# The low parts of a decoder trunk's attention weights subtracted on VectorE instead of GpSimd

## The chip, the cores and the metric

The kernel runs on one core of one Trainium2 chip. The metric is device microseconds of one execution; three executions of the kernel before took 1800.78 us in the median (1799.58 to 1805.04). The profiled execution is a run of its own. Engine names are those of the profile: PE is the matrix engine, PEld its weight loads, DVE is VectorE, ACT is ScalarE, POOL is GpSimd, SP is the queue that issues most DMAs.

## The reference, cut to what matters

Two layers over 1024 tokens of width 1024, all float32: an RWKV-7 layer and a differential-attention layer, each followed by a gated per-layer embedding, and a last RMSNorm. The change touches the attention layer:

```python
def diff_attn_mixer(h, w_in, lq1, lk1, lq2, lk2, subln, w_out, lambda_init):
    proj = h @ w_in                                   # q, k, v and gate of 8 heads
    q, k, v, gate = jnp.split(proj, [...], axis=-1)
    q, k = rope(q, cos, sin), rope(k, cos, sin)
    def block(args):                                  # 128 queries
        s = jnp.einsum('bhcqd,bhckd->bhcqk', qi, kt) * scale
        pr = jax.nn.softmax(causal(s), axis=-1)       # two maps per head
        att = pr[:, :, 0] - lam * pr[:, :, 1]
        return jnp.einsum('bhqk,bhkd->bhqd', att, vt)
    o = rms_norm(o, subln, DA_SUBLN_EPS) * (1.0 - lambda_init)
    return (o.reshape(B, S, DA_WIDTH) * jax.nn.silu(gate)) @ w_out
```

## The kernel before, in words

Every large product is computed in three matmuls of a rounded format (`mm3`): each operand x is split into a high part h, which ACT rounds by a copy, and a remainder x - h, which a second engine subtracts; then h·h, h·l and l·h are added in PSUM. The function `split(hi, lo, src, lo_eng)` does it: one ACT copy, and one subtraction on `lo_eng` (POOL where none is named). The subtraction reads two tensors of SBUF, the source and the high part.

The attention part works in nine passes of eight steps (`step(ph, ah, i)`). Pass `ph` projects head `ph`, 128 tokens a step (`pmm`: 24 matmuls of 512 columns into a tile called `qkv`, in two halves), while the head before, `ah = ph - 1`, goes through scores (`sc`), exponentials (`e`), the two maps' combination (`combine`, again `e`), transposition (`at`, evicted to SBUF by DVE as `aT`), the product with the values (`av`), and norms (`finish`, small rows on a 128x2 tile `ost`). Each step also rotates q and k (`rp`, `rq`: two rows on DVE, the rest on POOL), scales the gate (`sg`) and transposes q and k (`qkt`). The last pass, 8, has no projection; it loads the output projection's rows (`dwo`) and multiplies with them (`do`).

The weights of a head are four rows of 128x1024 (`dw` followed by head and row: dw43r is the raw row 3 of head 4, without the r the split one), the output projection has eight (`dwo0r` to `dwo7r`). Raw rows have two buffers (`RAW`), so the DMA of a row starts when the subtraction of the row two before it has ended. Head 0's rows are split in the last step of the stage before (the list `dw0`); the rows 0, 1 and 2 of head `ph + 1` are loaded in steps 2 to 4 of pass `ph` and row 3 in its last step (`wload2`); the rows of the output projection are loaded at the same places of the last two passes (`wo_row`). In the order that results, the four splits of a head run together at the end of one pass and the beginning of the next: row 3 of one head, then rows 0, 1 and 2 of the head after it.

The stage before the attention ends with `post2` of the last token tile: rows called `ple07th`, `h1b`, `da6`, `da7` and `n2r`, and the transposed and split activations `hT`. At the attention's start five small loads are issued on SP behind the write of `h1b`, among them `lamt`, from which a scalar `nlam` is computed on DVE.

The order of the instructions on each engine in this part is not the order of the code: a list scheduler inside the tile framework sets it, from its own model of durations and from priorities by program order, so a change of an engine moves other rows as well. Each engine then runs its own list in order.

Of the kernel before, what the change touches and what calls it, by code (L numbers as in the profile page):

```python
# [37 lines left out]
def trunk(ctx: ExitStack, tc: tile.TileContext, A, out):  # L38
# [17 lines left out]
    V, S, G, T = engines = [Engine(e) for e in (nc.vector, nc.scalar, nc.gpsimd, nc.tensor)]  # L56
# [29 lines left out]
    def split(hi, lo, src, lo_eng=None):  # L86
        S.activation(hi, src, AF.Copy)
        (lo_eng or G).tensor_tensor(out=lo, in0=src, in1=hi.bitcast(F32), op=ALU.subtract)
# [644 lines left out]
    def slot(nm):  # L733

        q = nslot[0] % RB
        nslot[0] += 1
        if q < 4:
            t = tip.tile([P, 2, D], F32R, tag=f"ti{q}", name=nm)
        else:
            t = de.tile([P, 2, D], F32R, tag="r", name=nm, bufs=RB - 4)  # L740
        return t[:, 0], t[:, 1]

    def wrow(nm, src, own=None, scale=None, lo_eng=None, raw=None, load=True):
        r = de.tile([P, D], F32, tag="raw", name=nm + "r", bufs=RAW) if raw is None else raw
        if load:
            nc.sync.dma_start(out=r, in_=src)
        if own is None:
            h, lo = slot(nm)
        else:
            h, lo = own  # L750
        if scale is None:
            split(h, lo, r, lo_eng)
        elif lo_eng is not None:
            S.activation(r, r, AF.Copy, scale=scale)
            split(h, lo, r, lo_eng)
        else:
            S.activation(h, r, AF.Copy, scale=scale)
            V.scalar_tensor_tensor(out=lo, in0=r, scalar=scale, in1=h.bitcast(F32), op0=ALU.mult, op1=ALU.subtract)
        return h, lo
# [86 lines left out]
    RB, RAW = 7, 2  # L846
# [6 lines left out]
    def big(kt, x, nm, dt=F32R):  # L853
        return dw.tile([P, D], dt, tag=f"b{kt}{x}", name=nm, bufs=1)

    with NB("d") as d, NP("psco") as pp:
# [108 lines left out]
        def wo_row(kt):  # L965
            r = wo_raw.pop(kt)
            h, lo = big(kt, 0, f"rwo{kt}h"), big(kt, 1, f"rwo{kt}l")
            split(h, lo, r, V)
            wo[kt] = (h, lo)
# [123 lines left out]
        for c in range(NCH):  # L1093
            i, odd = (c - 2) // 2, c % 2
# [39 lines left out]
            if c == 1:  # L1134
                wo_row(0)
            if c == 2:
                wo_row(5)
# [87 lines left out]
        def pre2(i):  # L1225
            h1 = d2.tile([P, D], F32, tag="h", name=f"h1b{i}", bufs=3)
            nc.sync.dma_start(out=h1, in_=h1_d[i * P:(i + 1) * P, :])
            for cs in GS:
                if i == cs.start:
                    RS[0] = group_rs(rn.rearrange("p c h j -> p c (h j)"), ss1, cs)  # L1230
            rs = RS[0][:, i:i + 1]
            n = dt_("y", f"n{i}", 3) if i < 2 else dt_("sg" if i % 2 else "xr", f"n{i}")
            V.tensor_scalar(out=n, in0=h1, scalar1=rs, scalar2=None, op0=ALU.mult)
            gh = kview(dt_("gh", f"ph{i}", 2, F32R))
            gl = kview(dt_("gl", f"pl{i}", 2, F32R))
            transpose_split(pp, f"ptr{i}", n, lambda hf: gh[:, hf * 4:hf * 4 + 4], lambda hf: gl[:, hf * 4:hf * 4 + 4],
                            tag="t")
            D2[i] = (h1, gh, gl)

        def mms2(i):  # L1240
            h1, gh, gl = D2[i]
            def tick(n, j=i - 2):
                if j > 0 and j % 2 and n in TT and n2p[j]:
                    kp = n2p[j].pop(0)
                    turn2(j, pp, "us", (D2[j - 1], D2[j]), [kp])
            D2[i] = (h1, proj_N(pp, f"pg{i}", gh, gl, wg, ("xy", "mm")[i % 2], 2, i == NT - 1, tick=tick))

        def post2(i):
            h1, pss = D2[i]
            rows = slice(i * P, (i + 1) * P)  # L1250
            ss = ple_tail(lambda tag, nm: dt_(tag, nm), d, f"ple0{i}", pss, h1, pp_d[0][rows, :])
            nc.sync.dma_start(out=h2_d[rows, :], in_=h1)
            rs = rms_rs(d, f"da{i}", ss, D, 1e-6)
            if i == NT - 2:
                nring.extend(t.bitcast(F32) for t in slot("n2r"))
            n2 = dt_("y", f"n2{i}", 3) if i < NT - 2 else nring[i - NT + 2]
            V.tensor_scalar(out=n2, in0=h1, scalar1=rs, scalar2=None, op0=ALU.mult)
            D2[i] = n2
# [39 lines left out]
        dw0 = []  # L1298
        TT = (2, 4, 6, 8)
        n2p = {j: list(range(KT // 2)) for j in (1, 3, 5)}  # L1300
        for i in range(1, NT):
            mms2(i)
            if i == NT - 1:
                for k4 in range(4):
                    hh, ll = slot(f"dw0{k4}")
                    split(hh, ll, dw0[k4], (G, G, V, G)[k4])
                    dw0[k4] = (hh, ll)
            if i + 2 < NT:
                pre2(i + 2)
            post2(i)  # L1310
            if i == NT - 3:
                dw0 = [de.tile([P, D], F32, tag="raw", name=f"dw0{k4}r", bufs=RAW) for k4 in range(2)]
                dw0 += [dt_("lnw", "dw02r"), dt_("y", "dw03r", 3)]
                for k4 in range(4):
                    nc.sync.dma_start(out=dw0[k4], in_=A["dqkvg"][0, k4])
# [5 lines left out]
    with tc.tile_pool(name="at", bufs=1, reuse_waits="tile") as at, tc.tile_pool(name="psat", bufs=1, space=PSUM, reuse_waits="tile") as pp:  # L1321
# [26 lines left out]
        def wload2(h, k4, lo_eng):  # L1348
            r = de.tile([P, D], F32, tag="raw", name=f"dw{h}{k4}r", bufs=RAW)
            nc.sync.dma_start(out=r, in_=A["dqkvg"][h, k4])  # L1350
            hh, ll = slot(f"dw{h}{k4}")
            split(hh, ll, r, lo_eng)
            H[h]["w"].append((hh, ll))
# [146 lines left out]

        def wo_row(kt):
            wo.append(wrow(f"dwo{kt}", A["dwo"][:, kt],
                           None if kt < RB else (big(0, 0, "dwo7h"), big(0, 1, "dwo7l")), lo_eng=V if kt in (4, 6) else G))

        def eturn(i):
            og = big(1, i % 2, f"og{i}", F32)
# [14 lines left out]
        def emm(i, hf):  # L1521
            gh, gl = EE[i]
            cs = slice(hf * 512, hf * 512 + 512)
            ps = pp.tile([P, 512], F32, tag="mm", name=f"do{i}{hf}", bufs=2)
            for kt in range(7):
                mm3(ps, gh[:, kt], gl[:, kt], wo[kt][0][:, cs], wo[kt][1][:, cs], kt == 0, kt == 6)
            V.tensor_tensor(out=h3[i][:, cs], in0=ps, in1=h3[i][:, cs], op=ALU.add)
# [38 lines left out]
        def step(ph, ah, i):  # L1566

            last = ph == DH
            if ah >= 0:
                scores(ah, i)  # L1570
            if i == 0 and ph > 1 and not last:
                pend.pop(1)()
            if not last:
                pmm(ph, i, 0)
                if i == NT - 1 and ph + 1 < DH:
                    wload2(ph + 1, 3, V)
            else:
                for kt in ((3, 4, 5, 6), (7,))[i] if i < 2 else ():
                    wo_row(kt)
                if i:  # L1580
                    emm(i - 1, 0)
            late = pend[1:] + pend[:1] if last and i == 0 else pend[:]
            del pend[:]
            for f in late:
                f()
            if ah >= 0:
                combine(ah, i)
            if not last:
                pmm(ph, i, 1)
                if ph == 0 and i == 2:  # L1590
                    turn2(NT - 1, pp, "tr", n7)
                if i and i % 2 == 0:
                    qkt(ph, i - 2)
                if i == NT - 1:
                    pend.append(lambda: qkt(ph, i - 1))
                if 2 <= i < 5:
                    if ph + 1 < DH:
                        if i == 2:
                            head(ph + 1)
                        wload2(ph + 1, i - 2, G)  # L1600
                    else:
                        wo_row(i - 2)
            else:
                e7 = range(3 * i - 18, 3 * i - 15) if i >= 6 else ()
                for x in e7:
                    turn7(x)
                if i == 0:
                    eturn(0)
                else:
                    emm(i - 1, 1)  # L1610
                if i in (3, 5, 7):
                    gate_pair(len(wg1), {3: "k1", 5: "kv", 7: "k1"}[i])
                if i == 7:
                    gate_pair(3, "q1")
                for x in e7:
                    emm7(x)
                if i + 1 < NT:
                    eturn(i + 1)
            if ah >= 0:
                pend.append(lambda: values(ah, i))  # L1620
                if i % 2:
                    pend.append(lambda: finish(ah, i - 1, 2))
# [127 lines left out]
```

## Time and profile before

| | |
|---|---|
| three timed executions, median | 1800.78 us (1799.58 to 1805.04) |
| profiled execution | 1792.27 us |
| its span, first to last instruction | 1790.4 us |
| PE busy | 1676.9 us, 94% |
| DVE busy | 1272.1 us, 71% |
| ACT busy | 798.9 us, 45% |
| POOL busy | 609.0 us, 34% |
| chain that ended last | PE 63%, DVE 25%, issue 4%, ACT 4%, POOL 3%, DMA 1% |

Busy times are sums over an engine's instructions, so overlapping ones count once. "Idle before" in a row is the time in which the engine did nothing before that row, and behind the arrow stands what ended it. In the profile nearly all rows carry the line of one helper (L50), so they are told apart by the tiles that they write and read: `dw<-dw43r,dw` is the subtraction for row 3 of head 4, and the copy before it is `dw<-dw43r`. Buffer numbers are left out there. A matmul or transposition of plain float32 operands shows as two records. Matmul ends are modelled.

### The profile page before, as it was taken

The page shows a single profiled execution, that of the slowest core. Times are in us where ns is not written, and L with a number is a line of the kernel's source. Part 1 is how long each engine was busy: PE and PEld are TensorE (multiplying, and loading weights), DVE is VectorE, ACT ScalarE, POOL GpSimd, SP SyncE. Part 2 cuts the span into 40 slices and gives each one's busy share as a digit, 9 for nine tenths or more (in the row PEclk, how much of TensorE's full clock was granted, in tenths as well). Part 3 has the DMA queues.
Part 4 walks back from the last instruction along what each step waited for, and adds up shares of the span by engine and source line. Part 5 has one row for each costly group of instructions (what it writes and reads, how often), then busy time and mean ns, then how long its engine had stood idle before and what let it go on. Part 6 is the DMA issues. An engine that isn't in the chain of part 4 may idle for free.

```text
span 1790.4 us, 31127 instructions
## 1 busy us (share of the span) xinstructions
PE 1676.9 (94%) x11768; PEld 1391.3 (78%) x11768; DVE 1272.1 (71%) x2910; ACT 798.9 (45%) x1690; POOL 609.0 (34%) x647
## 2 busy tenths in 40 slices
PE   6899999898998989999899899899999999999998
PEld 5677778887677878887678778788888888777786
DVE  7865845698994476666756657887787887856665
ACT  6567743346344443334434344444444444444332
POOL 4433634224323455656300342332423323311200
PEclk9999999998898999999899999999999999999999
DMA  7115444434216553453523210110111101521122
GB/s 261 53 54 165 140 121 104 131 99 117 82 62 192 168 172 119 131 167 113 212 101 135 93 60 7 53 49 17 54 33 30 56 9 55 188 70 34 59 95 71
DMA packets 164404, 176.03 MB, mean 98 GB/s; under 512 B 74845, under 2 KB 127837, under 8 KB 164254
## 3 DMA queue, kind: packets, MB, share of 16 engines
q1 hardware_dynamic: 161950, 169.84, 30.6%
q10 hardware_dynamic: 2304, 4.20, 0.6%
q8 instruction: 93, 1.52, 0.4%
q14 instruction: 57, 0.47, 0.1%
HBM read 124.19 MB, written 49.81 MB: 97 GB/s over the span
## 4 chain that ended last, share of the span: by engine, by line
PE 63%; DVE 25%; issue 4%; ACT 4%; POOL 3%; DMA 1%; SPq 0%; ACTq 0%; DVEq 0%; POOLq 0%
PE qkv L50 18%; PE d L50 7%; PE fg L50 5%; PE pg L50 5%; PE do L50 4%; PE sc L50 3%; DVE xmt L50 3%; PE xy L50 3%; PE av L50 3%; DVE tm L50 3%; PE op L50 3%; DVE tb L50 3%; DVE nb L50 2%; DVE ost L50 2%; PE pm L50 1%
## 5 line engine op out<-in xcount | busy, mean ns | idle before, releaser
L50 ACT ACTIVATE e<-sc,mx 128x256 f32<-128x256 f32 (+7 forms) x128 | 94.1, 739 | 110.7 <-DVE mx L50 59.7
L50 POOL TENSOR_TENSOR rp<-rp,rq 128x128 f32<-128x128 f32 x128 | 61.7, 503 | 227.8 <-DVE rq L50 173.8
L50 PE MATMUL sc<-k,q 128*128 128x512 f32 (+2 forms) x384 | 88.7, 363 | 3.8 <-ACT e L50 2.2
L50 PE MATMUL av<-vh,aT 128*128 128x128 f32 x576 | 81.2, 281 | 6.3 <-DVE aT L50 6.3
L50 PEld LDWEIGHTS av<-vh,aT 128*128 128x128 f32 x576 | 75.6, 195 | 12.8 <-DVE aT L50 8.9
L50 POOL TENSOR_TENSOR m<-m,mmask 128x512 f32<-128x512 f32 x32 | 47.9, 1496 | 81.7 <-ACT m L50 81.7
L50 DVE TENSOR_REDUCE mxs<-sc 128x1 f32<-128x128 f32 (+6 forms) x112 | 73.9, 680 | 0.5
L50 PEld LDWEIGHTS sc<-k,q 128*128 128x128 f32 x384 | 63.2, 190 | 12.9 <-ACT e L50 3.0
L50 PE MATMUL pg<-pwg,ph 128*128 128x512 f32 x224 | 73.2, 405 | 0.0
L50 PE MATMUL do<-dwo,oh 128*128 128x512 f32 x224 | 71.7, 401 | 0.8 <-DVE h L50 0.6
L50 DVE SCALAR_TENSOR_TENSOR xmt<-hT,cB,xmt 128x512 f32<-128x512 f32 x64 | 63.6, 1011 | 6.2 <-ACT xmt L50 5.8
L50 ACT ACTIVATE o<-av,r 128x128 f32<-128x128 f32 x64 | 23.5, 368 | 90.1 <-PE av L50 89.9
L50 DVE TENSOR_TENSOR tm<-tb,nb 128x31 f32<-128x31 f32 (+15 forms) x124 | 57.1, 461 | 3.6
L50 DVE SCALAR_TENSOR_TENSOR e<-e,r,e 128x128 f32<-128x128 f32 (+3 forms) x64 | 56.7, 887 | 1.2
L50 POOL CAST q<-q 64x128 fp32r<-64x128 f32 x128 | 38.8, 304 | 52.2 <-PE sc L50 48.0
L50 POOL CAST k<-k 64x256 fp32r<-64x256 f32 x64 | 25.7, 401 | 84.6 <-ACT k L50 83.5
L50 DVE TENSOR_TENSOR tb<-tb,tm 128x31 f32<-128x31 f32 (+15 forms) x124 | 51.8, 417 | 3.6
L50 DVE TENSOR_TENSOR rp<-qkv,rc 128x256 f32<-128x256 f32 x64 | 27.0, 421 | 36.7 <-PE qkv L50 34.0
L50 DVE COPY aT<-at 128x512 f32<-128x512 f32 (+2 forms) x96 | 51.8, 549 | 1.1 <-PE at L50 0.4
L50 PE MATMUL at<-ident,e 128*128 128x128 f32 x288 | 47.4, 277 | 3.1 <-DVE e L50 2.6
L50 DVE SCALAR_TENSOR_TENSOR ost<-ost 128x2 f32<-128x2 f32 x192 | 47.4, 247 | 3.8
L50 DVE TENSOR_TENSOR m<-pm,mmask 128x512 f32<-128x512 f32 x32 | 22.1, 691 | 38.2 <-PE pm L50 38.1
(1136 smaller groups left out, 5602.7 us busy)
## 6 DMA issues: line engine op xcount, KB each, us to landing
pp_d<-ppo SPq DMA_DIRECT2D x32, 256.0 KB, 2.5
kb_d<-kb SPq DMA_DIRECT2D x16, 512.0 KB, 3.3
kkr<-kkr_d SPq DMA_DIRECT2D x32, 256.0 KB, 3.8
kb<-kb_d SPq DMA_DIRECT2D x32, 256.0 KB, 3.5
x<-in_x SPq DMA_DIRECT2D x8, 512.0 KB, 5.8
kkr_d<-ep SPq DMA_DIRECT2D x16, 256.0 KB, 2.6
kkr_d<-rt SPq DMA_DIRECT2D x16, 256.0 KB, 2.6
bb<-kb_d SPq DMA_DIRECT2D x32, 128.0 KB, 2.9
```

What stands on the lines that cost most here:

```text
L50: r = f(*a, **k)
```

## The change

Of the 40 split weight rows of the attention (32 of the projections, 8 of the output projection) DVE subtracted 10 and POOL 30: three of head 0, three of each of seven other heads, six of the output projection. Now DVE subtracts all 40. Copies, loads, tiles and buffers are the same.

```diff
@@ last step of the stage before the attention
                 for k4 in range(4):
                     hh, ll = slot(f"dw0{k4}")
-                    split(hh, ll, dw0[k4], (G, G, V, G)[k4])
+                    split(hh, ll, dw0[k4], V)
                     dw0[k4] = (hh, ll)
@@ def wo_row(kt), rows of the output projection
             wo.append(wrow(f"dwo{kt}", A["dwo"][:, kt],
-                           None if kt < RB else (big(0, 0, "dwo7h"), big(0, 1, "dwo7l")), lo_eng=V if kt in (4, 6) else G))
+                           None if kt < RB else (big(0, 0, "dwo7h"), big(0, 1, "dwo7l")), lo_eng=V))
@@ def step(ph, ah, i)
                         if i == 2:
                             head(ph + 1)
-                        wload2(ph + 1, i - 2, G)
+                        wload2(ph + 1, i - 2, V)
                     else:
                         wo_row(i - 2)
```

The scheduler places the new rows among DVE's others and moves rows on PE, DVE, ACT and SP from the stage's last step on. First place: DVE where pass 3 ends and pass 4 begins, before the change. The tile `aT_12828` is the one for which PE's `av` waits there, `aT_12890` is the next transposition.

```order
L50 TENSOR_TENSOR dw_12814<-dw43r,dw_12814 128x1024
L50 SCALAR_TENSOR_TENSOR ost_10784<-ost_10784 128x2
L50 TENSOR_TENSOR ost_10784<-ost_10784 128x2
L50 SCALAR_TENSOR_TENSOR ost_10784<-ost_10784 128x2 x2
L50 COPY aT_12828<-at_12824 128x384
L50 TENSOR_TENSOR ost_10784<-ost_10784 128x2
L50 RECIPROCAL r_12957<-l_12868 128x2
L50 SCALAR_TENSOR_TENSOR ost_10784<-ost_10784 128x2
L50 SCALAR_TENSOR_TENSOR r_12957<-r_12957,l_12868,nlam 128x1
L50 SCALAR_TENSOR_TENSOR ost_10784<-ost_10784 128x2
L50 SCALAR_TENSOR_TENSOR e_12876<-e_12883,r_12957,e_12876 128x128
L50 TENSOR_SCALAR ost_10784<-ost_10784 128x2
```

Behind these come `rp`, two rows `o`, `rq` and then `aT_12890`. The same place on DVE with the change, from the same row on.

```order
L50 TENSOR_TENSOR dw_12814<-dw43r,dw_12814 128x1024
L50 SCALAR_TENSOR_TENSOR ost_10784<-ost_10784 128x2
L50 TENSOR_TENSOR dw_13163<-dw50r,dw_13163 128x1024
L50 SCALAR_TENSOR_TENSOR ost_10784<-ost_10784 128x2
L50 COPY aT_12828<-at_12824 128x384
L50 RECIPROCAL r_12957<-l_12868 128x2
L50 TENSOR_TENSOR ost_10784<-ost_10784 128x2
L50 TENSOR_TENSOR rp_12858<-qkv_12799,rc 128x256
L50 TENSOR_TENSOR rq_12859<-qkv_12799,rsn 128x256
L50 SCALAR_TENSOR_TENSOR r_12957<-r_12957,l_12868,nlam 128x1
L50 SCALAR_TENSOR_TENSOR ost_10784<-ost_10784 128x2
L50 COPY aT_12890<-at_12885 128x512
```

The subtraction of dw50r now stands ahead of `aT_12828`, the rows `rp` and `rq` stand ahead of `aT_12890`, and the two rows `o` have gone behind it; the subtractions of dw51r and dw52r come 9 and 15 rows after the last of these, behind the `sg` row that frees the `qkv` tile. Second place: PE at the same boundary with the change, where the second pair of `qkt` transpositions stood behind the matmuls of `hT4` before and now stands behind the first pair.

```order
L50 MATMUL av_12830<-vh_10783,aT_12828 128x128 x3
L50 MATMUL at_12892<-ident,e_12786 128x128 x4
L50 MATMUL qkt_12925<-ident,rp_12749 128x128 x2
L50 MATMUL qkt_12925<-ident,rp_12858 128x128 x2
L50 MATMUL av_12899<-vh_10783,aT_12890 128x128 x4
L50 MATMUL qkv_12912<-dw_12371,hT0h 128x512 x2
```

PE so needs the rotated tile `rp_12858`, which POOL finishes, before it begins the first projection of the pass. Third place: DVE at the end of the stage before the attention, before the change; the tiles `da6` are a row's norm, and `n2r` is scaled with it.

```order
L50 TENSOR_SCALAR da6r<-da6r 128x1
L50 SCALAR_TENSOR_TENSOR hT2l<-htr_10009,vecs,hT2h 128x256
L50 SCALAR_TENSOR_TENSOR da6t<-da6r,da6m 128x1
L50 SCALAR_TENSOR_TENSOR hT1l<-htr_9994,vecs,hT1h 128x256
L50 SCALAR_TENSOR_TENSOR da6r<-da6t,da6r 128x1
L50 SCALAR_TENSOR_TENSOR da6t<-da6r,da6m 128x1
L50 SCALAR_TENSOR_TENSOR da6r<-da6t,da6r 128x1
L50 SCALAR_TENSOR_TENSOR hT3l<-htr_10009,vecs,hT3h 128x256
L50 SCALAR_TENSOR_TENSOR da6t<-da6r,da6m 128x1
L50 SCALAR_TENSOR_TENSOR da6r<-da6t,da6r 128x1
L50 TENSOR_SCALAR n2r<-h1b_9704,da6r 128x1024
L50 TENSOR_TENSOR dw_10078<-dw02r,dw_10078 128x1024
```

Behind these stand the `ple07th`, `hT` and `h1b` rows of the last tile. The same place with the change, behind the subtraction of dw00r and its `hT` rows:

```order
L50 TENSOR_SCALAR da6r<-da6r 128x1
L50 TENSOR_TENSOR dw_10075<-dw01r,dw_10075 128x1024
L50 SCALAR_TENSOR_TENSOR da6t<-da6r,da6m 128x1
L50 TENSOR_TENSOR dw_10078<-dw02r,dw_10078 128x1024
L50 SCALAR_TENSOR_TENSOR hT3l<-htr_10009,vecs,hT3h 128x256
L50 SCALAR_TENSOR_TENSOR da6r<-da6t,da6r 128x1
L50 TENSOR_TENSOR dw_10081<-dw03r,dw_10081 128x1024
L50 SCALAR_TENSOR_TENSOR da6t<-da6r,da6m 128x1
L50 TENSOR_TENSOR dw_10311<-dw10r,dw_10311 128x1024
L50 SCALAR_TENSOR_TENSOR da6r<-da6t,da6r 128x1
L50 TENSOR_TENSOR dw_10351<-dw11r,dw_10351 128x1024
L50 SCALAR_TENSOR_TENSOR ple07th<-ple07th,ple07pp 128x512
```

Six subtractions now stand ahead of the last tile's `ple07th` and `h1b` rows, where one did, and `n2r` has gone behind these.

## Rows read from the trace of the kernel before

**Rows 1.** Stretches of the span; columns as in the first line.
```profile
core 0: us, PE busy (x) PEld busy (x) DVE busy (x) ACT busy (x) POOL busy (x), PEclk, DMA share, GB/s
990.00:1019.00 29.00, 24.37 (x105) 19.20 (x104) 23.55 (x47) 13.13 (x27) 13.34 (x10) 0.94 0.42 143
1019.00:1041.00 22.00, 20.19 (x96) 16.21 (x96) 8.20 (x22) 7.09 (x21) 7.12 (x14) 1.00 0.07 25
1118.00:1133.00 15.00, 9.76 (x53) 8.60 (x52) 14.68 (x35) 7.02 (x18) 9.30 (x9) 0.78 0.36 113
1266.20:1274.20 8.00, 6.15 (x46) 5.38 (x45) 7.86 (x25) 3.51 (x9) 5.19 (x6) 1.00 0.44 147
1274.20:1335.80 61.60, 61.60 (x320) 51.71 (x319) 48.74 (x161) 27.24 (x84) 17.82 (x39) 1.00 0.08 24
1543.00:1569.00 26.00, 21.69 (x123) 16.99 (x122) 23.29 (x74) 14.50 (x37) 9.32 (x13) 1.00 0.86 318
```

**Rows 2.** PE's largest wait from 985 to 1570 us: total, times, longest.
```profile
PE qkt L50 <- DVE aT L50: 8.1, 6, 1.4
```

**Rows 3.** Timeline of DVE where pass 3 ends: start, duration, instruction.
```profile
1265.32 0.16 DVE L50 SCALAR_TENSOR_TENSOR ost<-ost 128x2 f32<-128x2 f32 x1
1265.40 1.22 DVE L50 TENSOR_TENSOR dw<-dw43r,dw 128x1024 fp32r<-128x1024 f32 x1
1266.54 2.33 DVE L50 SCALAR_TENSOR_TENSOR ost<-ost 128x2 f32<-128x2 f32 x1
...
1269.49 0.56 DVE L50 COPY aT<-at 128x384 f32<-128x384 f32 x1
...
1270.22 0.22 DVE L50 SCALAR_TENSOR_TENSOR r<-r,l,nlam 128x1 f32<-128x1 f32 x1
...
1272.01 0.68 DVE L50 COPY aT<-at 128x512 f32<-128x512 f32 x1
...
1275.49 2.32 DVE L50 SCALAR_TENSOR_TENSOR r<-r,l,nlam 128x1 f32<-128x1 f32 x1
```

**Rows 4.** POOL's subtractions there: duration in ns, start in us.
```profile
L50 POOL TENSOR_TENSOR dw<-dw50r,dw x1: 2718/2718/2718, 1266.1 to 1266.1; 128x1024 fp32r<-128x1024 f32 x1
L50 POOL TENSOR_TENSOR dw<-dw52r,dw x1: 2386/2386/2386, 1275.4 to 1275.4; 128x1024 fp32r<-128x1024 f32 x1
```

**Rows 5.** Timeline of PE in the same stretch.
```profile
1272.83 0.41 PE L50 MATMUL qkt<-ident,rp 128*128 128x128 f32 x2 [1.36 <-DVE aT L50]
```

**Rows 6.** Timeline of DVE as the attention begins.
```profile
999.89 2.33 DVE L50 SCALAR_TENSOR_TENSOR da6r<-da6t,da6r 128x1 f32<-128x1 f32 x1
1002.26 2.81 DVE L50 TENSOR_SCALAR n2r<-h1b,da6r 128x1024 f32<-128x1024 f32 x1
...
1009.11 0.67 DVE L50 SCALAR_TENSOR_TENSOR h1b<-ple07th,h1b 128x512 f32<-128x512 f32 x1
```

**Rows 7.** PE and SP there.
```profile
1006.26 0.50 PE L50 MATMUL qkv<-dw,hT4h 128*128 128x512 f32 x1 [2.92 <-DVE dw L50]
...
1012.78 0.33 SPq L1333 DMA_DIRECT2D lamt<-in_lam  x1
...
1018.25 0.73 PE L50 MATMUL qkv<-dw,hT0h 128*128 128x512 f32 x2 [1.70 <-DVE sg L50]
```

**Rows 8.** DVE, ACT, POOL and PE where pass 1 ends.
```profile
1120.00 2.32 DVE L50 SCALAR_TENSOR_TENSOR ost<-ost 128x2 f32<-128x2 f32 x1
...
1123.99 1.06 ACT L50 ACTIVATE dw<-dw31r 128x1024 fp32r<-128x1024 f32 x1
...
1125.28 3.37 DVE L50 SCALAR_TENSOR_TENSOR e<-e,r,e 128x1024 f32<-128x1024 f32 x1
...
1127.51 1.28 POOL L50 CAST q<-q 64x128 fp32r<-64x128 f32 x1
...
1128.70 1.97 PE L50 MATMUL at<-ident,e 128*128 128x128 f32 x8 [2.62 <-DVE e L50]
```

**Rows 9.** ACT's wait for a landing where pass 2 ends.
```profile
1198.92 1.06 ACT L50 ACTIVATE dw<-dw41r 128x1024 fp32r<-128x1024 f32 x1 [2.51 <-DMA dw41r<-in_dqkvg]
```

## The prediction

> **What bounds the kernel now.** I read the table of stretches first, cut at the places where the profile's list of waits names PE. Between two pass ends PE has no idle time at all: 61.60 us busy of 61.60, while DVE is busy for 48.7 [rows 1]. A faster DVE or POOL is worth nothing there. PE waits only in short stretches: 1.85 us (8.00 less 6.15) where pass 3 ends [rows 1], the same within 0.01 at the ends of passes 2, 4, 5 and 6 (five in all); 5.2 us where pass 1 ends, 4.6 as the attention begins, 1.8 shortly after, 4.3 in the last pass [rows 1]. Together that is 25.2 us, the most that this change can win apart from the clock. In these stretches DVE is full: 7.86 of 8.00, 14.68 of 15.00.
>
> The list of waits says what PE waits for: the eviction `aT` on DVE, 8.1 us in six waits for the `qkt` that takes the freed bank [rows 2], 1.36 us of the 1.85 at one pass end [rows 5].
>
> Then the timeline of DVE, for why `aT` is late. At 1266.54 a row `ost` on 128x2 elements takes 2.33 us, where the same row took 0.16 just before; at 1275.49 a row `r` on 128x1 takes 2.32, where one took 0.22 [rows 3]. Both lie inside a subtraction of POOL: dw50r runs from 1266.1 for 2.72 us, dw52r from 1275.4 for 2.39, and each stretched row ends as POOL's does [rows 4]. The pair stands at all five pass ends of this kind, and the first row of it lies ahead of `aT`. So a subtraction that is no concern of PE holds DVE up for 2.2 us at the moment when PE needs DVE. The same lies over `n2r`, 2.81 us, and `da6r`, 2.33 [rows 6], and over `ost` and `e` where pass 1 ends [rows 8].
>
> **The change part by part.** Removed: 30 subtractions of 2.35 to 2.7 us on POOL [rows 4], and with them the stretches. Added: 30 on DVE at 1.22 us each, of which the next row sees 1.14 (1265.40 to 1266.54) [rows 3]. DVE so gets 34.2 us of work. A pass end has three of them, 3.4 us, and loses 2.17 + 2.10 = 4.3 of stretch; with 9.3 as the attention begins, 6.4 where pass 1 ends and 3.4 in the last pass the 20 stretched rows make 40 us. What counts is what stands ahead of each eviction.
>
> *Ends of passes 3 to 6, four times.* The order shows `ost`, the subtraction of dw50r, `ost`, then `aT`. From 1266.54: 0.20 + 1.14 + 0.20 puts the first `aT` at 1268.1 instead of 1269.49 [rows 3], and PE's wait for it (the other 0.49 of the 1.85) is gone. For the second `aT`, `rp` and `rq` now stand ahead, the two `o` rows no longer do: 1268.1 + 0.48 + some 1.4 for seven rows gives 1270.0 instead of 1272.01, with up to half a microsecond more if POOL's rotation holds the small rows up. PE reaches that `qkt` at about 1271.0 (1272.83 less 1.36 less 0.49 [rows 5]), so the 1.36 goes too, but for 0.2. The other two subtractions stand behind `sg`, which frees the next projection's bank: PE has 24 matmuls ahead of it by then. The early second `qkt` needs POOL's rotation, which ends at about 1270.6; it costs 0 to 0.3. I take 1.65 a pass end, 6.6 us.
>
> *End of pass 2.* The same, but dw41r stands ahead of `sg` there, and it comes only after its copy, which waited for a landing until 1198.92 [rows 9]. The projection then starts about 0.9 us late. I take 0.8 of 1.85.
>
> *End of pass 1.* `ost` loses 2.2, dw30r adds 1.14; `e`, 3.37 us long, loses a stretch of the same kind, some 2.1, and nothing stands in its place [rows 8]. So `e` ends at about 1125.4 instead of 1128.65. PE waited 2.62 us for it at 1128.70 [rows 8]; what is late next is the copy of dw31r at 1123.99, which waits for a landing and holds the exponential behind it. I take 3.0 of the 5.2.
>
> *As the attention begins.* Six subtractions instead of one now stand ahead of `h1b`: 5 x 1.14 = 5.7 us more. Five stretched rows go, together 9.3 us, with `n2r` and `da6r` [rows 6] the largest, and `n2r` moves behind. `h1b` at 1009.11 ends about 4 us earlier, and so do the loads on SP behind it, `lamt` at 1012.78 among them, on which PE's third projection at 1018.25 hangs through `sg`. PE's stall at 1006.26 (2.92) goes, but a wait for `lamt` of about 2.3 us stays [rows 7]. I take 3.7, from 0 (the copy of dw11r may land late, and its subtraction stands ahead of `h1b`) to 4.6.
>
> *Shortly after* (1019 to 1041): `qkt` moves ahead of a projection and the scores find their operands ready; 1.0 of the idle 1.8 [rows 1].
>
> *End of pass 0:* PE does not wait there, and DVE's spare time hides the four subtractions; they cost 0, or 1.1 if one comes late and stands before the rows that free a bank.
>
> *Last pass:* three subtractions add 3.4 us to a stretch in which DVE is busy for 23.3 of 26.0 [rows 1]; two of them stand ahead of score and `do` operands for which PE waits, and would cost 2.3. At most the idle 4.3 can be won. I take 0, between the two.
>
> Sum: 6.6 + 0.8 + 3.0 + 3.7 + 1.0 = 15.1 us. The profiled execution took 1792.27 us, 1.9 more than its span; it becomes 1777.2. The timed median, 1800.78, lies 8.5 above that execution, and I carry the difference over: 1786.
>
> *The clock.* Where PE had waited, the granted clock was below full in the next microseconds: 0.78 over the 15 us where pass 1 ends, 0.94 as the attention begins, 1.00 at the other pass ends of the rows [rows 1]. That is up to 3.3 and 1.7 us of PE time. If the waits go, some of it may come back; none is in the sum.
>
> *A rule weighed.* POOL's rows are held up as well: a `q` cast took 1.28 us beside the end of the stretched `e` [rows 8]. The new subtractions can do that to POOL's casts and rotations, and can be held up by them. The Trainium skill (SBUF — State Buffer, Who interferes with whom) says that the port pair is an exclusive lock between a DVE instruction with two SBUF inputs and a GpSimd one that reads SBUF, taken by whichever issues first. The stretched rows here agree, two-input ones all but `n2r`. By that rule each new row may wait behind a small POOL row, an estimate of at most 0.9 us (a rotation's two rows), and delay one by up to 1.1. I count neither: POOL's rows have microseconds of slack except the one `qkt` above.
>
> **The rivals.**
>
> *No change (within 5 us).* DVE only swaps 40 us of stretches for 34 of subtractions, and what PE waits for next is just behind: the landing of the middle rows. ACT's copy of dw41r waited 2.51 us for it [rows 9], and copies stand on ACT ahead of `o`, the casts and the exponentials. For it: DVE's busy time hardly falls. Against it: the stretch sits ahead of `aT` and the middle subtractions behind it. It would leave the pass ends at 1.85 and win only at the beginning: 0 to 5 us, 1796 to 1801. The Trainium skill (Perfetto Trace Analysis, Optimizing Scalar/DVE Operations) says the same in general: offloading between GpSimd and DVE might not help, since they share a port. By that rule this rival holds; the rows so far speak for the other, because POOL's subtraction takes 2.4 us and DVE's 1.2.
>
> *Slower.* DVE is the engine that ends PE's waits, and subtractions now stand ahead of `aT`, `sg` and `h1b`. If the small rows' 2.3 us were not POOL's doing, they stay, and each subtraction in front of an eviction adds 1.14 to a wait that is already there: one or two at seven pass ends (8 to 16 us) and five ahead of `h1b` (up to 5.7): 13 to 22 us, 1814 to 1823. It decides as soon as more than two subtractions precede the second `aT`, or a stretched row stays without a POOL row beside it. Against it: each stretched row ends with POOL's.
>
> *Much faster.* All idle time goes and the clock stays full: 25 + 5, 1771.
>
> **How the numbers follow.** The forecast 0.74 (its own range 1778 to 1794), no change 0.15, slower 0.06, much faster 0.05. A difference under 0.3%, 5.4 us, could not be told from none. Faster than 1795.4: the forecast but for a small tail, and the last case, 0.78. Slower than 1806.2: 0.07. Between: 0.15. The range leaves out the slower case, the upper end of no change, and the extreme win: 1775 to 1799.
>
> **What would show it.** Right: `ost` and `r` at the pass ends back at 0.16 and 0.22; DVE's busy time down by about 6 us, POOL's by 73; PE's idle time at the ends of passes 3 to 6 below 0.4 us; PE's waits for `aT` (8.1 us for `qkt`) under 2; `lamt` issued about 4 us earlier. Wrong step by step: `aT` at a pass end not earlier (the order would have eaten the gain), a long wait of PE on `sg` or `qkt` at every pass end (the middle subtractions or POOL's rotation late), or the last pass longer by over 2.4. Wrong altogether: rows of 2.3 us on DVE without a POOL subtraction beside them.

## The result, and the profile after

The changed kernel took 1775.8 us in the median (1772.86 to 1780.80; one disturbed run of 4070.86 us is left out), the kernel before 1800.18 us in the same series: 24.4 us between the medians where 15.1 were forecast. The ratio is 0.9884, 95% interval 0.986 to 0.9907, that is, 16.7 to 25.2 us; the forecast lies just below that. The profiled spans are 1770.7 and 1790.4 us, 19.7 apart. A second series of the same two kernels gave 0.987 (0.9847 to 0.9893).

These are the stretches of the changed kernel that answer to [rows 1]. It reaches the attention 2.8 us later and the end of the last pass 16.9 earlier, so the windows are shifted to the same work:

```profile
core 0: us, PE busy (x) PEld busy (x) DVE busy (x) ACT busy (x) POOL busy (x), PEclk, DMA share, GB/s
993.00:1022.00 29.00, 27.71 (x129) 22.30 (x128) 20.72 (x56) 14.20 (x30) 2.36 (x6) 1.00 0.44 143
1022.00:1044.00 22.00, 22.00 (x106) 18.03 (x105) 11.10 (x27) 7.48 (x23) 7.16 (x16) 1.00 0.08 25
1113.30:1128.30 15.00, 11.98 (x73) 10.09 (x72) 13.57 (x44) 8.27 (x22) 2.64 (x7) 1.00 0.44 149
1254.50:1262.50 8.00, 7.54 (x54) 6.77 (x53) 7.97 (x26) 4.00 (x12) 1.52 (x5) 1.00 0.44 138
1262.50:1324.10 61.60, 61.60 (x322) 51.85 (x321) 50.25 (x166) 26.95 (x84) 14.22 (x36) 1.00 0.08 26
1526.00:1552.00 26.00, 22.40 (x123) 17.95 (x122) 23.17 (x73) 16.06 (x38) 5.52 (x11) 0.93 0.91 334
```

PE's idle time at the end of pass 3 is 0.46 us (8.00 less 7.54) instead of 1.85, as the attention begins 1.29 instead of 4.6, where pass 1 ends 3.0 instead of 5.2. The granted clock is 1.00 in the two windows that had 0.94 and 0.78; the last pass, 1.00 before, now has 0.93.

DVE at the end of pass 3, beside [rows 3] (start, duration, instruction):

```profile
1255.13 1.22 DVE L50 TENSOR_TENSOR dw<-dw50r,dw 128x1024 fp32r<-128x1024 f32 x1
1256.26 0.15 DVE L50 SCALAR_TENSOR_TENSOR ost<-ost 128x2 f32<-128x2 f32 x1
1256.45 0.56 DVE L50 COPY aT<-at 128x384 f32<-128x384 f32 x1
...
1257.72 0.21 DVE L50 SCALAR_TENSOR_TENSOR r<-r,l,nlam 128x1 f32<-128x1 f32 x1
...
1257.91 0.68 DVE L50 COPY aT<-at 128x512 f32<-128x512 f32 x1
```

`ost` and `r` are back at 0.15 and 0.21 us, and between 988 and 1600 us no DVE row takes over 0.5 us more than the shortest of its kind; before, 20 did, 41 us together. PE's largest waits there, beside [rows 2] (total, times, longest):

```profile
PE sc L50 <- ACT e L50: 3.3, 4, 1.5
PE av L50 <- ACT o L50: 2.9, 5, 0.7
PE do L50 <- ACT oh L50: 1.7, 1, 1.7
PE av L50 <- DVE aT L50: 1.6, 3, 0.6
PE qkv L50 <- DVE sg L50: 1.3, 1, 1.3
```

The wait of `qkt` for `aT` (8.1 us [rows 2]) is gone. The first three that are left are for ACT. The timeline of ACT and PE shows why, at the end of pass 3 and of pass 1 (where the copy has taken the place of the long `e` of [rows 8]):

```profile
1118.92 1.06 ACT L50 ACTIVATE dw<-dw31r 128x1024 fp32r<-128x1024 f32 x1 [0.75 <-DMA dw31r<-in_dqkvg]
1119.88 0.35 ACT L50 ACTIVATE e<-sc,mx 128x128 f32<-128x128 f32 x1
...
1120.38 0.51 PE L50 MATMUL sc<-k,q 128*128 128x256 f32 x2 [1.50 <-ACT e L50]
...
1258.59 1.06 ACT L50 ACTIVATE dw<-dw51r 128x1024 fp32r<-128x1024 f32 x1 [0.26 <-DMA dw51r<-in_dqkvg]
1259.56 0.35 ACT L50 ACTIVATE o<-av,r 128x128 f32<-128x128 f32 x1
...
1259.95 1.16 PE L50 MATMUL av<-vh,aT 128*128 128x128 f32 x8 [0.46 <-ACT o L50]
```

The copy of a pass's second row waits on ACT for its landing, and the eviction `o` or the exponential `e` stands behind it. That is what is late next.

The table shows where the 19.7 us lie. All 11768 matmuls stand in both traces, so the time from the n-th to the m-th can be compared; idle is PE's time without a matmul in it, and the last stretch ends with the start of the last matmul.

| stretch (time before) | forecast gain | idle before, after | length before, after |
|---|---|---|---|
| start to 990 | 0 | | 990.20, 992.96 |
| 990 to 1041, attention begins and shortly after | 4.7 | 6.43, 1.29 | 50.86, 43.66 |
| 1041 to 1100 | 0 | 0.12, 0.11 | 59.16, 58.94 |
| 1100 to 1160, end of pass 1 | 3.0 | 5.24, 3.01 | 59.81, 55.48 |
| 1160 to 1230, end of pass 2 | 0.8 | 1.85, 0.69 | 70.03, 66.84 |
| 1230 to 1510, ends of passes 3 to 6 | 6.6 | 7.39, 2.34 | 279.96, 274.18 |
| 1510 to 1575, last pass | 0 | 4.31, 3.60 | 65.19, 66.27 |
| 990 to 1575 together | 15.1 | 25.3, 11.0 | 585.0, 565.4 |
| 1575 to the last matmul | 0 | 6.19, 5.09 | 206.42, 203.69 |

The idle time fell by 14.3 us, the forecast within 0.8. The length fell by 19.6. The other 5.3 are in the matmuls themselves, the same 2920 of them; first the kernel before, then the changed one:

```profile
990.20:1575.20 585.00, 559.67 (x2920) 467.54 (x2919) 452.43 (x1413) 256.04 (x741) 198.82 (x349) 0.99 0.17 56
```

```profile
992.96:1558.30 565.34, 554.31 (x2920) 465.54 (x2919) 450.45 (x1443) 257.23 (x742) 131.90 (x320) 1.00 0.18 59
```

PE is busy for 559.67 and 554.31 us, with a granted clock of 0.99 and 1.00. The clock falls to half of full speed, 1.2 of 2.4 GHz, in a few short places, each at the end of a wait of PE or just behind it. Before, there are three between 990 and 1575 us, as the attention begins and behind passes 1 and 2; after, there is one, in the last pass (three lines before, one after; PEclk is the column behind POOL's):

```profile
1007.00:1010.00 3.00, 3.00 (x8) 2.31 (x8) 3.00 (x7) 1.74 (x5) 0.00 (x0) 0.50 0.02 5
1127.00:1133.00 6.00, 4.29 (x19) 4.23 (x20) 5.85 (x13) 2.26 (x7) 3.48 (x4) 0.50 0.35 106
1202.00:1204.50 2.50, 2.50 (x12) 2.40 (x11) 1.65 (x8) 2.06 (x7) 2.50 (x2) 0.50 0.01 3
...
1540.00:1543.00 3.00, 2.96 (x10) 2.45 (x10) 3.00 (x11) 1.27 (x2) 0.03 (x1) 0.50 1.05 408
```

Half of the time that the trace shows at half clock is lost: 6.8 us before and 1.7 after, so the clock is 5.1 of the 5.3 us.

### The profile page after: what moved, and what is told of

It is laid out like the page before. It is cut to its first block, busy times and chain, and to the rows that moved or that the text cites. A ratio compares the mean times of both kernels' runs of the same rounds, so it can differ in the third digit from the quotient of the medians.

```text
span 1770.7 us, 31132 instructions
## 1 busy us (share of the span) xinstructions
PE 1674.5 (95%) x11768; PEld 1393.3 (79%) x11768; DVE 1269.7 (72%) x2940; ACT 797.5 (45%) x1690; POOL 538.8 (30%) x617
## 4 chain that ended last, share of the span: by engine, by line
PE 58%; DVE 26%; issue 5%; ACT 5%; POOL 3%; DMA 3%; SPq 0%; ACTq 0%; DVEq 0%; POOLq 0%
PE qkv L50 15%; PE d L50 6%; PE fg L50 5%; PE do L50 5%; PE pg L50 5%; DVE xmt L50 3%; PE xy L50 3%; DVE tm L50 3%; PE op L50 3%; DVE tb L50 3%; PE sc L50 3%; PE av L50 3%; DVE nb L50 2%; PE pm L50 1%; POOL m L50 1%
## 5 line engine op out<-in xcount | busy, mean ns | idle before, releaser
L50 POOL CAST k<-k 64x256 fp32r<-64x256 f32 x64 | 29.6, 462 | 130.3 <-ACT k L50 99.6
L50 ACT ACTIVATE o<-av,r 128x128 f32<-128x128 f32 x64 | 23.4, 366 | 97.9 <-PE av L50 97.8
L50 PEld LDWEIGHTS do<-dwo,oh 128*128 128x128 f32 x224 | 41.6, 191 | 11.7 <-ACT oh L50 2.0
L50 PEld LDWEIGHTS pg<-pwg,ph 128*128 128x128 f32 x224 | 42.3, 193 | 9.3 <-ACT ph L50 0.2
```

The lines of the kernel that those rows point to most:

```text
L50: r = f(*a, **k)
```

## The experiments

All ratios are against the kernel before; "length" and "idle" are taken as in the table above.

**Each part alone.** Three kernels with one of the three edits each, and one with a third of the largest.

```diff
-split(hh, ll, dw0[k4], (G, G, V, G)[k4])
+split(hh, ll, dw0[k4], V)                             # begin_only
-wload2(ph + 1, i - 2, G)
+wload2(ph + 1, i - 2, V)                              # passes_only
+wload2(ph + 1, i - 2, V if i == 2 else G)             # first_row
-lo_eng=V if kt in (4, 6) else G
+lo_eng=V                                              # last_only
```

> The kernel before, with only the three subtractions of dw00, dw01 and dw03 moved to DVE (as the attention begins). Theory (what counts is what stands ahead of an eviction; the stretch of two-input DVE rows beside POOL's subtractions is what is won): two of the stretched rows there go (da6t, 1.47 and 1.85 us over), three subtractions of 1.14 come ahead of h1b, so DVE gains almost nothing at h1b; the stretches beside dw10r and dw11r (da6r 2.33, n2r 2.81) stay. PE's 2.92 us wait for the remainder dw goes or shrinks, the wait for sg stays near 1.7. 0 to 4 us faster, I take 2; the ends of passes 1 to 6 keep their waits (5.2 and five times 1.85) and the half-clock stretches behind passes 1 and 2 stay. Rival (the order as a whole, not the places, makes the gain): no stretch shorter, or pass ends changed as well.

> The kernel before, with only the 21 subtractions of the rows of heads 1 to 7 moved to DVE. Theory: all of the gain at the ends of passes 1 to 5 (in the two traces 4.3 + 3.2 + 4.4 us with the clock) and most of that as the attention begins (dw10r and dw11r stand there; 3 to 5 of 7.2): 14 to 18 us faster than before. The end of pass 6 keeps its 1.85 of idle time. Idle time of PE at the ends of passes 3 to 5 near 0.55, as in the changed kernel. No half-clock stretch behind passes 1 and 2. Rival (order as a whole): the parts do not add up, this one alone gives under 8 or the full 24.

> The kernel before, with only the six subtractions of the output projection's rows moved to DVE. Theory: three of them stand at the end of pass 6 (idle 1.85 becomes some 0.6), three in the last pass, where the two traces show idle time 4.3 against 3.6 and the same length but for a half-clock stretch: 1 us faster, from 3 faster to 2.4 slower; not distinguishable from no change in the timed runs. Everything before 1475 us stays as it was. Rival (subtractions ahead of do's and the scores' operands cost): 2 to 3 us slower in the last pass.

> The kernel before, with only the first of the three rows per pass moved to DVE (dw10r, dw20r, ..., dw70r: seven subtractions). Theory: this is the row whose POOL subtraction holds the ost ahead of aT, so at the ends of passes 3 to 5 PE's idle time falls from 1.85 to about 0.55, the r row beside the third subtraction still takes 2.3 us and costs PE nothing. At the end of pass 1 ost is back at 0.16 but e still takes 3.4, so about half of the 5.2 stays. In time 7 to 11 us faster than before, over half of what all 21 give. Rival (every stretched row counts alike): a third of it, 5 us, with 1.2 of idle time at each pass end. Rival (order, not the stretch): nothing.

| | before | begin_only | passes_only | last_only | first_row | changed |
|---|---|---|---|---|---|---|
| ratio | | 0.9989 | 0.9931 | 0.9984 | 0.9982 | 0.9884 |
| 95% interval | | 0.9975 to 1.0004 | 0.9906 to 0.9956 | 0.9965 to 1.0002 | 0.9965 to 0.9999 | 0.986 to 0.9907 |
| 990 to 1041 | 50.86 | 50.59 | 49.41 | 51.33 | 51.44 | 43.66 |
| 1100 to 1160, end of pass 1 | 59.81 | 60.08 | 57.04 | 60.45 | 59.74 | 55.48 |
| 1160 to 1440, ends of 2 to 5 | 280.1 | 280.1 | 273.6 | 279.0 | 275.4 | 272.5 |
| its idle time | 7.39 | 7.36 | 3.46 | 7.56 | 4.09 | 2.33 |
| 1440 to 1510, end of pass 6 | 69.88 | 71.47 | 70.00 | 68.50 | 69.91 | 68.54 |
| 990 to the last matmul | 791.4 | 791.9 | 781.1 | 789.4 | 787.4 | 769.1 |

The timed runs alone do not tell `begin_only` and `last_only` from no change; the places have to be read from the traces. They are as expected: the 21 rows of the passes work at the ends of passes 1 to 5 and not at that of pass 6, the six output rows work there. The first row alone gives 4.7 of the 6.5 us that all 21 give at the ends of passes 2 to 5, and nothing at the end of pass 1, where other stretched rows (one `ost` of 2.35 us ahead of an `aT`) kept PE waiting. Neither 7 to 11 us for it nor 14 to 18 for the 21 came (4.0 and 10.3 from 990 on): both miss the beginning. The parts alone add to some 12 us of length, all together give 22. Of the missing 10, 6 lie between 990 and 1041, where the first two edits alone give 0.3 and 1.5, the third loses 0.5, and all give 7.2. PE's waits there, in the kernels with the first edit alone, the second alone, and all:

```profile
1016.80 1.22 PE L50 MATMUL qkv<-dw,hT0h 128*128 128x512 f32 x2 [3.67 <-DVE sg L50]
...
1040.05 0.35 PE L50 MATMUL sc<-k,q 128*128 128x256 f32 x1 [1.61 <-DVE q L50]
```

```profile
1021.91 0.73 PE L50 MATMUL qkv<-dw,hT0h 128*128 128x512 f32 x2 [3.13 <-DVE sg L50]
...
1044.18 0.36 PE L50 MATMUL sc<-k,q 128*128 128x256 f32 x1 [1.61 <-DVE q L50]
```

```profile
1010.72 0.42 SPq L1333 DMA_DIRECT2D lamt<-in_lam  x1
...
1015.98 0.74 PE L50 MATMUL qkv<-dw,hT0h 128*128 128x512 f32 x2 [1.29 <-DVE sg L50]
```

Beside [rows 7]: either edit alone takes away PE's stall for the remainder (2.92), and PE then stands some 2 or 1.4 us longer at `sg`, which hangs on `lamt`. (That the wait for `sg` would stay near 1.7 with the first edit was a miss.) Counted from the same matmul (at 990.20 before), `lamt` is issued after 22.6 us before, 20.0 and 20.4 with one edit, 17.8 with all. PE's two waits add to 4.62 us before, 3.67 and 3.13 with one edit, 1.29 with all: each edit alone mostly moves the stall from the second projection to the third. The wait of 1.61 for `q`, which is there before the change too, is still there with each edit alone and gone in the order that the scheduler makes of all edits.

The clock has the larger part in the missing 10. From 990 to 1575 PE loses 6.8 us to half clock before, 10.2, 3.4 and 8.5 with one edit alone, and 1.7 with all: in this the three parts together fall 6.8 us short of the whole. In idle time they fall 4.3 short (10.0 against 14.3), 3.0 of it between 990 and 1041. `passes_only` still has a half-clock stretch behind pass 1, where none was expected.

**Is it POOL's reading, or POOL's queue?** The changed kernel, with a needless piece of POOL work behind each moved subtraction, on the raw row that is dead by then: the same subtraction, or three fills that together take about as long (2.43 us).

```diff
 split(hh, ll, r, V)                                                     # 30 places
+G.tensor_tensor(out=r, in0=r, in1=hh.bitcast(F32), op=ALU.subtract)     # dummy_sub
+G.memset(r, 0.0); G.memset(r, 0.0); G.memset(r[:, 0:512], 0.0)          # dummy_set
```

> The changed kernel, and behind each of the 30 moved subtractions POOL does one of the same shape that nobody needs (raw row minus its rounded copy, written over the raw row, which is dead by then). DVE's order stays that of the changed kernel; POOL is as busy as before. Theory (two-input DVE rows wait while POOL's subtraction reads SBUF): two-input rows of 0.15 to 0.4 us take some 2.3 again right behind the subtractions, PE's idle time at the ends of passes 2 to 6 goes from 0.5 to 0.7 back to 1.5 or more, and since DVE now has its own 1.14 us as well, the stretch from 990 us to the end is as long as before or up to 12 us longer: 1796 to 1812 in the timed runs, nothing left of the gain. Rival (the gain is DVE's order, or that the remainder is ready sooner): as the changed kernel, 1774 to 1780.

> As the run with the needless subtractions, but POOL fills the dead raw row with zeros instead (two and a half fills of 128x1024, some 2.4 us, which write SBUF and read nothing). Theory (it is POOL's reading of SBUF, not its being busy, that holds DVE's two-input rows): no stretched rows, idle time at the pass ends as in the changed kernel, 0.5 to 0.8; 1774 to 1782. Rival (any POOL work on SBUF holds DVE, or the gain is POOL's free queue for the rotations and casts): as with the needless subtractions, no faster than before.

Measured: 1.0063 (1.0043 to 1.0082) with the subtractions, 0.9919 (0.9895 to 0.9942) with the fills; the median times were 1807.93 and 1780.48 us. Lengths at the ends of passes 2 to 5: 283.5 and 273.2 (before 280.1, changed 272.5); idle time at each of the ends 2 to 6: 1.9 to 2.7 and 0.3 to 0.9. DVE and POOL at the end of pass 3, with the subtractions and then with the fills:

```profile
1275.14 1.22 DVE L50 TENSOR_TENSOR dw<-dw50r,dw 128x1024 fp32r<-128x1024 f32 x1
...
1276.49 2.35 POOL L50 TENSOR_TENSOR dw50r<-dw50r,dw 128x1024 f32<-128x1024 f32 x1 [3.79 <-issue]
1277.00 1.86 DVE L50 TENSOR_TENSOR ost<-ost 128x2 f32<-128x2 f32 x1
...
1279.61 0.87 POOL L50 TENSOR_TENSOR rp<-rp,rq 128x128 f32<-128x128 f32 x2 [0.76 <-DVE rq L50]
...
1280.47 0.41 PE L50 MATMUL qkt<-ident,rp 128*128 128x128 f32 x2 [1.42 <-POOL rp L50]
```

```profile
1261.77 1.22 DVE L50 TENSOR_TENSOR dw<-dw50r,dw 128x1024 fp32r<-128x1024 f32 x1
...
1263.09 1.97 POOL L50 MEMSET dw50r<- 128x1024 f32 x2 [3.76 <-issue]
1263.63 0.14 DVE L50 TENSOR_TENSOR ost<-ost 128x2 f32<-128x2 f32 x1
```

The same row, at the same place of the same order: 1.86 us beside a subtraction on POOL, ending as that ends, 0.14 beside a fill. POOL is as busy in both (613.2 and 612.0 us). DVE's order did not stay that of the changed kernel everywhere, as the expectation has it; around the rows shown, from the subtraction of dw43r to that of dw51r, it is the same in all three kernels. PE waits here for POOL's rotation `rp`, which looks like POOL's queue. But POOL had been idle for 0.76 us before that row, until DVE's `rq` ended, and `rq` stands behind the stretched `ost`; it is so at the ends of passes 3 to 6 alike. So at the pass ends it is POOL reading SBUF that holds DVE, and the rival, POOL's free queue or DVE's order, falls. At the beginning of the attention the subtractions cost more (58.26 from 990 to 1041), and the fills cost as well (50.74, as before the change) though no row there is stretched: `lamt` is issued after 20.0 us with them instead of 17.8, and PE waits 4.80 us for `sg`. Why the dead rows hold that up was not followed.

**What is late next.** Two changes of the changed kernel: the rounded copies of each pass's second row taken on POOL, or `lamt` loaded and reduced long before.

```diff
-split(hh, ll, r, lo_eng)                              # in wload2: pool_copy
+if k4 == 1:
+    G.tensor_copy(hh, r)
+    V.tensor_tensor(out=ll, in0=r, in1=hh.bitcast(F32), op=ALU.subtract)
+else:
+    split(hh, ll, r, lo_eng)
...
-lamt = at.tile([P, 4, L], F32, tag="rp2", name="lamt", bufs=2)          # lam_early
+lamt = de.tile([P, D], F32, tag="raw", name="lamt", bufs=RAW)[:, 0:4 * L]   # ahead of the gate rows
```

> The changed kernel, with the rounded copy of each pass's second row (dw11r, dw21r, ..., dw71r) taken on POOL instead of ACT. Theory (what is late next at a pass end is this copy: it waits on ACT for its landing, and the eviction o or the exponential stands behind it): PE's idle time of 0.46 to 0.70 at the ends of passes 2 to 6 falls to 0.3 or less, the two waits for e at the end of pass 1 (1.50 and 0.95) lose at least 1 us together; 2 to 4 us faster than the changed kernel from 990 us on. Rival (a POOL copy reads SBUF, so it holds DVE's two-input rows as the subtractions did, and DVE's own subtraction queues behind it): idle time of 1 us or more at those pass ends, slower than the changed kernel by 3 to 8 us.

> The changed kernel, with lamt loaded and reduced at the start of the gate stage instead of as the attention begins. Theory (the third projection hangs on sg, which stands on DVE behind lamt's rows, and those behind a load issued after h1b's store): the wait of 1.29 us for sg at 1015.98 falls below 0.4, the stretch from 990 to 1041 gets about 1 us shorter, the rest stays. Rival (the loads of the rotation tables, issued between h1b's store and lamt, land just as late): no difference.

The copies on POOL: 0.9873 (0.985 to 0.9897), in the timed runs no more than the changed kernel has, where the trace is 5.8 us shorter from 990 on (763.3 against 769.1). PE's idle time at the ends of passes 2 to 5 is 0.03 us each, and the length from 1160 to 1440 is 270.3 us instead of 272.5. Where pass 1 ends, the waits of 1.50 and 0.95 for ACT's `e` became one of 0.93, but one of 0.83 for DVE's `e` came. The copy takes 1.04 us there, and two DVE rows beside such a copy were held by 0.7 and 0.85. So what had been left at the ends of passes 2 to 5 was the copy that waited on ACT with `o` behind it. `lamt` early: 0.9912 (0.9892 to 0.9932). Its wait of 1.29 went, as expected, but the length from 990 to 1041 grew from 43.66 to 44.24, for a wait came back:

```profile
1040.77 0.36 PE L50 MATMUL sc<-k,q 128*128 128x256 f32 x1 [1.61 <-DVE q L50]
```

The step was right and the gain was nothing, because the scheduler's order changed again.

**A faster version, and how far the rule carries.** In one series: the changed kernel again, POOL copies for dwo1 and dwo5 too, and with these the remainders of the gate projections' rows on DVE (`GE` and the engine of `gate_pair`).

> The changed kernel once more, for comparison in the same series. Both theories: 0.986 to 0.991 of the time before; from 990 us to the end about 769 us in the trace, idle time of 0.46 to 0.70 at the ends of passes 2 to 6 (up to 1.6 where a landing comes late).

> The changed kernel with the rounded copies of the second row of each pass and of dwo1 and dwo5 on POOL instead of ACT. Theory (the copy that waits on ACT for its landing holds o, oh and the exponentials): besides the five pass ends, which were idle for 0.03 us each with the heads' rows alone, the end of pass 6 (0.90) falls below 0.3 and the wait for oh in the last pass (1.28 to 1.67) loses some 1 us; 5 to 8 us faster than the changed kernel from 990 us on. Rival (the timed runs, which differ by 2.5 us between the two so far, show that the trace's 5.8 us were that run's clock): no more than 2 us faster than the changed kernel, a tie within the interval.

> The same, and the remainders of the gate projections' rows, which POOL still takes, on DVE as well. Theory (a subtraction on POOL holds the DVE row beside it wherever it stands): rn, 2.31 us beside the subtraction of pwg07r at 881.6, and the ost rows, 2.26, beside those of pwg14r and pwg15r at 1655 and 1657, go back to 0.2; the waits of PE just behind them, 3.27 us for n at 885.20 and 3.26 for o at 1661.28, lose 2 to 2.3 each; DVE's own 1.2 us rows cost up to 1 there: 2 to 4 us faster than the run without the gate rows. Rival (those waits are a chain of small rows on DVE that POOL has no part in): no difference, or slower by the 1.14 us of each row that comes ahead of n or o.

Medians 1773.26, 1767.46 and 1770.49 us; ratios 0.987 (0.9847 to 0.9893), 0.9843 (0.9817 to 0.9868), 0.985 (0.9826 to 0.9874). The middle one has the lowest median here, 5.8 us under the changed kernel, and its trace is shorter by as much (764.6 against 770.2 from 990 on, the 5 to 8 that the theory expected). The timed intervals overlap, and the trace with the heads' copies alone was no longer (763.3), so what the copies of dwo1 and dwo5 add to the whole is not shown. The end of pass 6 is idle for 0.02 us, the wait for `oh` went from 1.76 to 0.67. Pass 3's end in it:

```profile
1251.60:1259.60 8.00, 7.97 (x53) 6.98 (x53) 7.72 (x27) 3.42 (x12) 2.44 (x5) 1.00 0.40 132
```

With the gate rows on DVE, the wait for `o` got shorter, 3.26 us in the kernel without them to 2.12, and another came; first that kernel, `pool_copy_wo`, then the one with the gate rows:

```profile
1653.97 0.71 PE L50 MATMUL o<-ident,o 128*128 128x128 f32 x2 [3.26 <-DVE o L50]
1654.87 0.79 PE L50 MATMUL do<-dwo7h,g 128*128 128x512 f32 x1 [0.19 <-ACT g L50]
```

```profile
1661.49 0.56 PE L50 MATMUL o<-ident,o 128*128 128x128 f32 x2 [2.12 <-DVE o L50]
...
1665.04 0.80 PE L50 MATMUL do<-dwo7h,g 128*128 128x512 f32 x1 [2.99 <-ACT g L50]
```

The other wait named, for `n`, shows nothing: it was 2.37 us without and 2.42 with the gate rows, and 1.91 to 3.29 in kernels that do the same work there. So neither theory holds as put: POOL had a part in the wait for `o`, and freeing DVE did not free the chain.

## Why the prediction was right, and where it was too small

*The mechanism* was right: the stretched rows were POOL's doing (the two needless pieces of work show it), the first of them at a pass end is the one that counts (the first row alone gives 4.7 of 6.5 us), and the subtractions in front of the evictions cost less than the stretches did. The Trainium skill (SBUF — State Buffer, Who interferes with whom) says that an instruction of DVE with two SBUF inputs contends with one of GpSimd that reads SBUF, and not with one that only writes it; the rows of 1.86 and 0.14 us agree with both halves.

*The number* was met by little. 1775.8 us lies 0.8 above the lower end of the range (1775 to 1799), below the forecast's own range (1778 to 1794), and nearer to the rival "much faster" (1771) than to 1786; that it falls in the range at all is partly luck. That rival's condition did not hold, for 11.0 of the 25.3 us of idle time are left. Of the 10 us between forecast and result 5.3 are the clock and 5.6 the offset from the span to the timed median, while the idle time gave 0.8 less than forecast.

*The clock* is the term that was mis-sized: "none is in the sum". It makes up the difference between 990 and 1575, 5.3 us. The prediction had worked out what the waits cost by the clock in two stretches, 3.3 and 1.7 us, and both came back; the 1.7 behind pass 2, which it did not see, came back too, and 1.7 were lost anew in the last pass. All kernels, over the same 2920 matmuls, show that busy time goes by the time at half clock ("lost" is half of that time, from the traces):

| kernel | PE idle | PE busy | lost |
|---|---|---|---|
| dummy_sub | 34.1 | 563.5 | 11.9 |
| before | 25.3 | 559.7 | 6.8 |
| begin_only | 24.3 | 562.3 | 10.2 |
| last_only | 23.4 | 561.0 | 8.5 |
| first_row | 21.9 | 560.4 | 8.5 |
| passes_only | 18.2 | 557.7 | 3.4 |
| dummy_set | 14.2 | 555.4 | 1.7 |
| lam_early | 13.4 | 554.5 | 1.7 |
| changed_again | 12.2 | 553.0 | 0 |
| changed | 11.0 | 554.3 | 1.7 |
| pool_copy | 7.7 | 552.1 | 0 |
| pool_copy_gates | 7.5 | 557.2 | 5.1 |
| pool_copy_wo | 6.0 | 552.3 | 0 |

Busy time less the lost part is 551.6 to 554.3 us in all thirteen. With the idle time it goes only on average: from the first row to the last 28.1 us less idle time come with 11.2 us less busy time, some 0.4 us for each microsecond of waiting, but `pool_copy_gates` loses 5.1 us with hardly more idle time than `pool_copy_wo`, which loses none. Before the change PE waits 1.85 us at each of five pass ends, and the clock falls behind one of them, that of pass 2; what decides it is open. In `last_only` that place stays at full clock, and the end of pass 2 is 1.5 us shorter with the same wait.

*Ends of passes 3 to 6*: 6.6 forecast, 5.05 of idle time, 5.8 in length (no half clock lies there in either trace). The 1.36 for the second `aT` went entirely. The sum had the 0.49 for the first `aT` gone as well. It went, but a wait of 0.46 to 0.70 for `o` has its place, behind the copy of the middle row, so the idle time is not below the 0.4 forecast. That is the mechanism of "no change", at a third of its price. *End of pass 2*: 0.8 forecast, 1.16 idle. *End of pass 1*: 3.0 forecast, 2.2 idle; `e` is back at 1.27 us, and the copy of dw31r, named as next, holds an exponential for which PE waits 1.50. *The beginning and shortly after*: 4.7 forecast, 5.1 idle. `lamt` came 4.8 us earlier (4 forecast), and the wait for `sg` is 1.29, not 2.3. *The last pass*: nothing forecast, 0.7 less idle time, but 1.1 longer, for the clock lost 1.7 there.

*Busy times*: POOL's fell by 70.2 us (73 forecast), DVE's by 2.4, not 6.

*From the span to the timed median*: the offset of 8.5 us was carried over; after the change it was 2.9 (1775.8 less 1772.86). That part is not shown to be the change's: in the eleven profiled runs whose work before the attention is untouched, that part ended between 990.2 and 1000.8 us, and the kernel before had the shortest. The lengths from 990 on, 22.4 us apart and 21.3 in the second trace, are the firmer measure; the timed medians gave 24.4 and 21.3.

## What to carry to other kernels

Look for rows that take a multiple of their usual time and end together with a row of another engine; what they cost is what stands behind them in the queue, so one such row ahead of an eviction is worth more than several elsewhere. Price the clock too: look up where the trace shows half clock, see which waits stand ahead of those places, and put what they lose into the sum if these waits go. And before adding parts, follow each stall to the next one: an edit that frees one of two chains wins little until the other is freed.

## What the runs showed of the hardware that was not expected

A fill on POOL, which reads nothing, holds DVE's one-source `TENSOR_SCALAR` rows on 128x2 elements. With the fills, eleven such `ost` rows (six of float32, five of int32) that began beside a fill took 0.45 to 0.97 us, where 0.15 is usual, and each ended 0.02 us after the fill; a twelfth took 0.28. The 16 two-source `ost` rows, twelve `r` and six `o` beside fills kept their 0.14 to 0.35, and so did five `TENSOR_SCALAR` rows on 128x1 (0.14 to 0.15). Three `TENSOR_SCALAR` rows behind one another, of which the last two (0.97 and 0.92) met a fill, and POOL beside them:

```profile
1136.00 2.11 DVE L50 TENSOR_SCALAR ost<-ost 128x2 f32<-128x2 f32 x3
...
1136.18 0.95 POOL L50 MEMSET dw32r<- 128x1024 f32 x1
...
1137.56 0.52 POOL L50 MEMSET dw32r<- 128x512 f32 x1
```

The stretched rows of the kernel before that have one source, `n2r` [rows 6] and an `ost` row in the last pass that the prediction's "all but `n2r`" leaves out (1.40 us at 1558.45, ending with the subtraction of dwo5r), fit this second kind; no run has `n2r` beside a fill. The Trainium skill (SBUF — State Buffer, Who interferes with whom) has it: `tensor_scalar` can enter a mode that takes both ports, and then contends with any GpSimd work on SBUF; the 128x2 rows beside fills agree.

A rounding copy of 128x1024 on POOL took 1.04 or 1.05 us in five of the seven rows of `pool_copy` (1.32 and 1.96 in the others) against 2.4 for a subtraction of that shape, and 1.06 on ACT. It held DVE rows too, by at most 0.85 us against 2.2, so here the copy was the piece of a split that POOL could take at the lower cost to DVE.
